# Two attentions reordered: later transpositions in the dilated one, queries, keys, values in the sparse one

## The chip, the cores and the metric

The kernel runs on one core of a Trainium2 chip, as one program. The metric is the device time of one execution in microseconds (us). The engines are called as the profile calls them: PE is TensorE's matrix multiplication and PEld its weight load, DVE is VectorE, ACT is ScalarE, POOL is GpSimd, SP is SyncE, which issues the loads.

## The reference

One sequence of 512 tokens, width 1024, passes through two layers of one kind and one of another, all in float32.

- First kind, twice: `x += 0.5*swiglu(norm(x))`, a mixing part, again `x += 0.5*swiglu(norm(x))`. The mixing part projects to queries, keys and values of 12 heads of 64 and to a pooled part. Each head attends with a mixture of three dilated windows, whose weights come out as one softmax over all 512 keys with a bias by distance:

```
num = sum(wts[i][..., None] * branches[i][0] for i in range(len(branches)))
den = sum(wts[i] * branches[i][2] for i in range(len(branches)))
return (num / den[..., None]).astype(q.dtype)
```

- Second kind, once: a gated MLP over chunks of 128 tokens (`gmlp`), and a sparse attention of 8 heads with 2 groups of keys. That has three outputs, mixed by gates: attention to 31 compressed blocks (each made from 32 keys or values by a small MLP, `cmp_k_w1`, `cmp_k_w2` and the same for v), to selected blocks, and to a window:

```
g = jax.nn.sigmoid(g_raw + gate_b).reshape(B, S, N_GATES, N_KV, GQA, 1)
o = g[:, :, 0] * o_cmp + g[:, :, 1] * o_slc + g[:, :, 2] * o_win
```

With 8 blocks in all and 16 to be selected, every block is selected, so the second and third come out as plain causal attention with different keys and values. A feed-forward and a norm follow.

## The kernel before

Every float32 product is made of three matmuls of rounded halves: `wh*xh + wh*xl + wl*xh` (`mm3`, lines 409 to 413). So each weight tile ("unit", up to 128 x 1024) is loaded by SP (line 305), copied to a rounded high part `wh` by ACT (line 368), and its remainder `wl` is made by DVE (line 375). `unit()` takes the next unit in a fixed list and first splits ahead so that two more are ready; raw tiles, `wh` and `wl` have three buffers each. The list is written in `stages()`, and its order must be that in which the code takes the units. Engines get their instructions in the order that the framework's scheduler works out from the program's order and from what is ready; each engine then runs its own list.

Dilated attention, `mix()` (lines 825 to 1070), called for each of the first two layers: 12 heads of 4 query tiles give 48 tiles, and one loop over steps t (line 1054) runs a software pipeline over them. Step t does the score product of tile t (`qk_step`, line 773 by way of `scores`), normalises tile t-1 (`norm_step`: a reciprocal on DVE and a multiplication on POOL, line 1010), adds the output product of tile t-LP (`pv_step`, line 1034), transposes tile t-LT on PE (`turn_step`, line 1016: four 128 x 128 blocks from the four probability tiles of a head, with the high part copied by ACT, line 1018), takes the softmax of tile t (`exp_step`: DVE line 1003, ACT line 1004) and makes the low part of the transposed tile (`low_step`, line 1023). The first transposition of a head needs the probabilities of all its four tiles. Beside it `beside()` yields small pieces of other projections (late queries, keys and values, then half of the output projection, `out_part`), of which each step takes one or two (line 1067). The probabilities lie in tiles of the tag `work`, of which there are NP.

Sparse attention, `mix2()` (lines 1073 to 1544): in the pool `cm` the kernel projects the inputs of compression (`two_first`), four tiles of queries (`one`, `fill_q`), the keys `ks` and `kw` (`fill_k`), and the values with the gates (`wide`, line 1222); between them `hidden()` (line 1186) yields the pieces of the compression MLP, four units for the keys and four for the values. `blocks()` prepares its inputs `blkh`, `blkl` on POOL, ACT and DVE. Then small weights are loaded and split: `w2` (line 1233, splits in 1235 and 1236) and `ws` with the triangular mask `tril` (lines 1239 to 1244). The pool `cm` closes, a pool `at` opens, and the loop over 64 tiles runs as in `mix()`, with its softmax in line 1277 (DVE), its scores in line 773 and its own LT, LP = 5, 7.

Of the kernel before, what the change touches and what calls it, by code (L numbers as in the profile page):

```python
# [23 lines left out]
ALU = mybir.AluOpType  # L24
AX = mybir.AxisListType

P = 128
# [5 lines left out]
TC = S // P  # L33
# [55 lines left out]
def _u(w, k0, nk, c0, nc):  # L89

    return w[k0 * P : (k0 + nk) * P, c0 : c0 + nc].reshape(nk, P, nc).transpose(1, 0, 2).reshape(P, nk * nc)
# [32 lines left out]
def ffn_units(wg, wu, wd):  # L124
    for t in ffn_plan():
        if len(t) == 2:
            pairs = PHASES[t[0]]
            yield "D", [_u(wd, 2 * pairs[0], 2 * len(pairs), t[1] * P, P)]
        else:
            yield t[2], [  # L130
                np.concatenate([_u(w, 4 * j, 4, (2 * t[1] + i) * P, P) for w in (wg, wu)], 1)
                for i, j in BLOCKS.get(t[2], ())
            ]


def out_units(w):
    for k0 in (0, 4):
        for c0 in range(0, D, 256):
            yield _u(w, k0, 4, c0, 256)


def wide_units(w):
    for k in range(0, 8, 2):
        yield _u(w, k, 2, 0, 512)


def stages(i):
    for l in range(2):
        yield from ffn_units(i["ffn1_w_gate"][l], i["ffn1_w_up"][l], i["ffn1_w_down"][l])
        w = i["w_in"][l]  # L150
        q, k, v = (w[:, 256 + 768 * j : 1024 + 768 * j] for j in range(3))
        yield from wide_units(q[:, :512])
        yield from wide_units(k[:, :512])
        yield _u(w, 0, 8, 0, P)
        yield _u(w, 0, 8, P, P)
        yield from wide_units(v[:, :512])
        for m in (q, k, v):
            yield _u(m, 0, 4, 512, 256)
            yield _u(m, 4, 4, 512, 256)
        yield from out_units(i["w_out"][l])  # L160
        yield from ffn_units(i["ffn2_w_gate"][l], i["ffn2_w_up"][l], i["ffn2_w_down"][l])


    w = i["w_in_2"][0]
    cmp = [_u(i[f"cmp_{n}_w1_2"][0], k0, 4, 0, 256) for n in "kv" for k0 in range(0, 16, 4)]
    q = _by_kv(w[:, 1024:1536])
    v = np.concatenate([w[:, 1920:2048], w[:, 2176:2328]], 1)
    yield from (_u(w, 0, 8, c0, P) for c0 in (1536, 1664))
    yield from (_u(q, 0, 8, j * P, P) for j in range(3))
    yield cmp[0]  # L170
    yield _u(q, 0, 8, 3 * P, P)
    yield cmp[1]
    yield _u(w, 0, 8, 1792, P)
    yield cmp[2]
    yield _u(w, 0, 8, 2048, P)
    yield cmp[3]
    for n, (k0, nk) in enumerate(((0, 3), (3, 3), (6, 2))):
        yield _u(v, k0, nk, 0, 280)
        yield cmp[4 + n]
    yield cmp[7]  # L180
    for c0 in (512, 768, 0, 256):
        yield _u(w, 0, 4, c0, 256)
        yield _u(w, 4, 4, c0, 256)
    wo = i["w_o_2"][0]
    yield from out_units(np.concatenate([wo[:512], _by_kv(wo[512:].T).T]))
    yield from ffn_units(i["w_gate_2"][0], i["w_up_2"][0], i["w_down_2"][0])
# [41 lines left out]
def tile_blocks(tc, A, out):  # L228
    nc = tc.nc
    V, ACT, G, PE = nc.vector, nc.scalar, nc.gpsimd, nc.tensor  # L230

    with (
# [458 lines left out]
        def wide(ncol, kper, after_first=None, between=None):  # L691
            o = [bank() for _ in range(TC)]
            got = None
            for k0 in range(0, KC, kper):
                u = unit()
                for k in range(k0, min(k0 + kper, KC)):
                    c0 = (k - k0) * ncol
                    for t in range(TC):
                        tok = slice(t * P, (t + 1) * P)
                        mm3(o[t][:, :ncol], cut(pair[k], slice(None), tok),  # L700
                            cut(u, slice(None), slice(c0, c0 + ncol)), k == 0, k == KC - 1)
                if k0 == 0 and after_first:
                    got = after_first()
                if between:
                    between()
            return (o, got) if after_first else o
# [69 lines left out]
        def fill_v(dst, src, r):  # L776

            h, l = dst[:, :, 0, :], dst[:, :, 1, :]
            if r is None:
                ACT.activation(h, src, AF.Copy)  # L780
                return low_of(l, src, h)
            else:
                ACT.activation(h, src, AF.Copy, scale=r)
                return V.scalar_tensor_tensor(l, src, r, h.bitcast(F32), op0=ALU.mult, op1=ALU.subtract)
# [39 lines left out]

        def mix(l, nxt):
            with tc.tile_pool(name="mix", bufs=2) as pool:
                NP = 8

                def work(name):
                    return pool.tile([P, 640], F32, name=name, tag="work", bufs=NP)[:, :544]  # L830

# [89 lines left out]
                o, r = wide(512, 2, lambda: row_factor(sums["s"], D, "rf"))  # L921
# [15 lines left out]
                o = wide(512, 2, between=turns(st_q, "q", NQ))  # L937
# [4 lines left out]
                o, mark = wide(512, 2, lambda: state["low"], turns(st_k, "k", NK))  # L942
# [43 lines left out]

                NH = 12
                TURN = 2
                LT, LP = 5, 7
                prob, pt, outp, den = {}, {}, {}, {}  # L990

                def qk_step(t):
# [61 lines left out]
                for t in range(NS + LP):  # L1054
                    if t < NS:
                        sc = qk_step(t)
                    if 0 <= t - 1 < NS:
                        norm_step(t - 1)
                    if 0 <= t - LP < NS:
                        pv_step(t - LP)  # L1060
                    if 0 <= t - LT < NS:
                        turned = turn_step(t - LT)
                    if t < NS:
                        exp_step(t, sc)
                    if 0 <= t - LT < NS:
                        low_step(t - LT, *turned)
                    for _ in range(2 if t < 20 else 1 + (t % 3 == 0)):
                        next(side, None)
                run(side)
                run(out_part(4, second))  # L1070
# [2 lines left out]
        def mix2(nxt):  # L1073
            with tc.tile_pool(name="mix2", bufs=2) as pool:
# [13 lines left out]
                vsw = pool.tile([P, TC, 4, 2, HD], F32R, name="vsw", bufs=1)  # L1088
                gate = pool.tile([P, P], F32, name="gate", bufs=1)[:, : TC * 24].rearrange("p (a b) -> p a b", a=TC)
                caus = pool.tile([P, S], F32, name="caus", bufs=1)  # L1090
                cmpb = pool.tile([P, TC, 32], F32, name="cmpb", bufs=1)
                gateb = pool.tile([P, P], F32, name="gateb", bufs=1)[:, :24]
# [44 lines left out]
                with tc.tile_pool(name="cm", bufs=1) as cm:  # L1137
# [6 lines left out]
                    rho = small.tile([P, TC], F32, name="rho", tag="rfac", bufs=6)  # L1144
# [35 lines left out]
                    blk = blocks(tk, 0)  # L1180
# [5 lines left out]
                    def hidden(b, got):  # L1186

                        o = bank("hid")
                        for k0 in range(0, 16, 4):
                            w = unit()  # L1190
                            for m in range(k0, k0 + 4):
                                mm3(o[0:62, :256], cut(b, slice(None), m), cut(w, slice(None), slice((m - k0) * 256, (m - k0 + 1) * 256)),
                                    m == 0, m == 15)
                            if k0 < 12:
                                yield
                        h = pool.tile([P, 256], F32, name="hid", tag="hid", bufs=2)[0:62]
                        gelu(h, o[0:62, :256], 0.5, 0.5 * c1, work("gq")[0:62, :256])
                        got.append(h)
                        yield
# [11 lines left out]

                    hid = []
                    pieces = hidden(blk, hid)
                    next(pieces)
                    fill_q(qt[3], scaled(one(), rb, -0.125))
                    next(pieces)
                    blk = blocks(tv, 1)
                    for kind in "sw":
                        fill_k(kt[kind], scaled(one(), rb), ACT.copy)
                        next(pieces)  # L1220
                    pieces = hidden(blk, hid)
                    o = wide(280, 3, between=lambda: next(pieces))
                    for t in range(TC):
                        r = rho[:, t : t + 1]
                        fill_v(vsw[:, t], o[t][:, :256].rearrange("p (h d) -> p h d", h=4), r)
                        V.scalar_tensor_tensor(gate[:, t, :], o[t][:, 256:280], r, gateb, op0=ALU.mult, op1=ALU.add)
                    next(pieces)
                    hk, hv = hid

                    tril = cm.tile([P, P], F32, name="tril")  # L1230
                    nc.sync.dma_start(tril, A["consts"][:, C_TRIL : C_TRIL + P])
# [2 lines left out]
                    w = w2.rearrange("p (a b c) -> p a b c", a=2, b=2)  # L1234
                    ACT.activation(w2s[0], w, AF.Copy)
                    V.tensor_sub(w2s[1], w, w2s[0].bitcast(F32))
                    for j in range(2):
# [3 lines left out]
                        w = ws.rearrange("p (a b) -> p a b", a=4)  # L1241
                        V.tensor_tensor(w, w, tril.unsqueeze(1).to_broadcast([P, 4, P]), op=ALU.mult)
                        ACT.activation(wss[0][:, hs], w, AF.Copy)
                        V.tensor_sub(wss[1][:, hs], w, wss[0][:, hs].bitcast(F32))

                    ACT.activation(gate, gate, AF.Tanh, scale=0.5)
                    V.tensor_scalar(gate, gate, 0.5, 0.5, op0=ALU.mult, op1=ALU.add)

# [2 lines left out]
                with tc.tile_pool(name="at", bufs=2) as at:  # L1251
                    KINDS = ("s", "w")
                    LT, LP = 5, 7
# [371 lines left out]
```

## Time and profile before

| | us |
|---|---|
| three runs | 2511.68, 2514.0, 2514.68 |
| median | 2514.0 |
| the profiled execution | 2511.51 |
| its span, first to last instruction | 2509.7 |
| PE busy | 2455.3 (98%) |
| DVE busy | 1970.6 (79%) |
| ACT busy | 1312.8 (52%) |
| POOL busy | 206.3 (8%) |
| DMA | 229.72 MB, mean 92 GB/s |

The busy times are of the one profiled execution. The granted clock of PE is 0.994 of full speed over the span. A "wait" is idle time of an engine just before an instruction, put down to the engine and line whose signal came last. In a timeline a row is an instruction, or several alike that follow each other (x3), with the start, the time from first start to last end, the engine, the line and the tiles (output<-inputs).

### The profile page before, as it was taken

How to read it: one execution, taken by the hardware profiler on the slowest of the kernel's cores; microseconds unless marked ns; L12 is line 12 of the kernel's file. 1: busy time of each engine (PE TensorE's matmuls, PEld its weight loads, DVE VectorE, ACT ScalarE, POOL GpSimd, SP SyncE). 2: the span in 40 equal slices, each digit the busy share in tenths (PEclk: the TensorE clock that was granted, in tenths of full speed). 3: DMA queues.
4: the chain of work that ended last, by engine and by line, in shares of the span. 5: the costliest groups of instructions: out<-in, count | busy, mean ns of one | idle time of the engine just before them, and what ended most of it. 6: DMA issues, size and time to landing. Idle time of an engine off the chain costs nothing.

```text
span 2509.7 us, 39707 instructions
## 1 busy us (share of the span) xinstructions
PE 2455.3 (98%) x15714; PEld 2216.4 (88%) x15714; DVE 1970.6 (79%) x2982; ACT 1312.8 (52%) x2061; POOL 206.3 (8%) x407
## 2 busy tenths in 40 slices
PE   7999999999999999999999999999999999999997
PEld 7999988887999989999988888999988887899996
DVE  8987764798977778877756789887776898987775
ACT  6544443676544455444444776444455775644442
POOL 0000004430000000000003430000000222000000
PEclk9999999999999999999999999999999999999999
DMA  4233232113333332333232113333233211333322
GB/s 178 93 105 101 79 103 84 60 43 105 92 115 105 100 103 84 112 105 101 77 91 84 43 44 116 110 99 106 74 100 108 88 43 43 118 94 109 104 63 78
DMA packets 73338, 229.72 MB, mean 92 GB/s; under 512 B 9536, under 2 KB 9920, under 8 KB 73152
## 3 DMA queue, kind: packets, MB, share of 16 engines
q1 hardware_dynamic: 73152, 227.19, 29.0%
q8 instruction: 123, 2.02, 0.3%
q14 instruction: 63, 0.52, 0.1%
HBM read 225.06 MB, written 2.10 MB: 91 GB/s over the span
## 4 chain that ended last, share of the span: by engine, by line
PE 88%; DVE 7%; ACT 2%; issue 1%; POOL 1%; DMA 1%; DVEq 0%; SPq 0%; ACTq 0%; POOLq 0%
PE x L633 13%; PE x L631 13%; PE x L632 13%; PE dn L411 8%; PE dn L412 8%; PE dn L413 8%; PE mm L411 6%; PE mm L413 6%; PE mm L412 6%; PE ov L1034 1%; DVE wl L375 1%; PE tp L1016 1%; PE mm L773 1%; PE mm L774 1%; PE ov L1323 1%
## 5 line engine op out<-in xcount | busy, mean ns | idle before, releaser
L631 PE MATMUL x<-rh,wh 128*128 128x256 f32 x1600 | 453.9, 284 | 3.2 <-ACT rh L446 2.3
L632 PE MATMUL x<-rl,wh 128*128 128x256 f32 x1600 | 454.3, 284 | 2.7 <-DVE rl L447 2.7
L633 PE MATMUL x<-rh,wl 128*128 128x256 f32 x1600 | 454.2, 284 | 0.7 <-DVE wl L375 0.7
L368 ACT ACTIVATE wh<-wd 128x768 fp32r<-128x768 f32 (+2 forms) x265 | 237.6, 896 | 352.8 <-PE x L632 178.3
L411 PE MATMUL dn<-ah,wh 128*128 128x512 f32 x880 | 343.9, 391 | 0.0
L412 PE MATMUL dn<-al,wh 128*128 128x512 f32 x880 | 343.8, 391 | 0.0
L631 PE MATMUL x<-yh,wh 128*128 128x256 f32 x1200 | 339.8, 283 | 4.0 <-DVE cc L572 3.3
L413 PE MATMUL dn<-ah,wl 128*128 128x512 f32 x880 | 342.3, 389 | 0.0
L633 PE MATMUL x<-yh,wl 128*128 128x256 f32 x1200 | 339.7, 283 | 0.0
L632 PE MATMUL x<-yl,wh 128*128 128x256 f32 x1200 | 339.6, 283 | 0.0
L368 ACT ACTIVATE wh<-wr 128x1024 fp32r<-128x1024 f32 (+1 forms) x178 | 187.6, 1054 | 250.7 <-PE x L632 87.0
L631 PEld LDWEIGHTS x<-rh,wh 128*128 128x128 f32 x1600 | 308.0, 193 | 6.0 <-ACT rh L446 2.5
L632 PEld LDWEIGHTS x<-rl,wh 128*128 128x128 f32 x1600 | 308.2, 193 | 5.4 <-DVE rl L447 3.1
L633 PEld LDWEIGHTS x<-rh,wl 128*128 128x128 f32 x1600 | 308.3, 193 | 1.1 <-DVE wl L375 1.1
L375 DVE TENSOR_TENSOR wl<-wd,wh 128x768 fp32r<-128x768 f32 (+2 forms) x265 | 270.4, 1020 | 43.3 <-ACT wh L368 40.1
L375 DVE TENSOR_TENSOR wl<-wr,wh 128x1024 fp32r<-128x1024 f32 (+1 forms) x178 | 218.5, 1228 | 79.8 <-ACT wh L368 79.1
L631 PEld LDWEIGHTS x<-yh,wh 128*128 128x128 f32 x1200 | 230.2, 192 | 7.9 <-DVE cc L572 4.6
L632 PEld LDWEIGHTS x<-yl,wh 128*128 128x128 f32 x1200 | 230.2, 192 | 2.2
L633 PEld LDWEIGHTS x<-yh,wl 128*128 128x128 f32 x1200 | 230.3, 192 | 0.0
L413 PEld LDWEIGHTS dn<-ah,wl 128*128 128x128 f32 x880 | 165.3, 188 | 35.2
L411 PEld LDWEIGHTS dn<-ah,wh 128*128 128x128 f32 x880 | 165.7, 188 | 31.3
L412 PEld LDWEIGHTS dn<-al,wh 128*128 128x128 f32 x880 | 165.7, 188 | 29.8
(326 smaller groups left out, 5151.1 us busy)
## 6 DMA issues: line engine op xcount, KB each, us to landing
wr<-in_w SPq DMA_DIRECT2D x175, 512.0 KB, 3.6
wd<-in_w SPq DMA_DIRECT2D x120, 384.0 KB, 3.1
wq<-in_w SPq DMA_DIRECT2D x78, 512.0 KB, 3.6
wd<-in_w SPq DMA_DIRECT2D x55, 512.0 KB, 3.6
wd<-in_w SPq DMA_DIRECT2D x40, 256.0 KB, 3.1
x<-in_xT SPq DMA_DIRECT2D x8, 256.0 KB, 6.2
out<-x SPq DMA_DIRECT2D x8, 256.0 KB, 2.0
bias<-in_consts SPq DMA_DIRECT2D x2, 448.0 KB, 3.9
```

The costliest lines, as they stand in the source:

```text
L368: ACT.activation(h[:, :n], src[:, :n], AF.Copy)
L375: state["low"] = V.tensor_sub(l[:, :n], src[:, :n], h[:, :n].bitcast(F32)).ins
L411: PE.matmul(o, w[0], xx[0], start=start, stop=False)
L412: PE.matmul(o, w[0], xx[1], start=False, stop=False)
L413: PE.matmul(o, w[1], xx[0], start=False, stop=stop)
L631: PE.matmul(oo, wh, xh, start=start and j == 0 and c == 0, stop=False, skip_group_check=True)
L632: PE.matmul(oo, wh, xl, start=False, stop=False, skip_group_check=True)
L633: PE.matmul(oo, wl, xh, start=False, stop=c == 3, skip_group_check=True)
L773: PE.matmul(o, q[g][:, cq], k[g][:, ck], start=True, stop=False)
L774: PE.matmul(o, q[g][:, cq], k[2 + g][:, ck], start=False, stop=True)
L1016: PE.transpose(o[:, i * P : (i + 1) * P], prob[h * TC + i][0][:, j * P : (j + 1) * P], ident)
L1034: PE.matmul(o, w, part, start=(j == 0 and n == 0), stop=(j == TC - 1 and n == 1))
```

## The change

In `mix()`: NP from 8 to 9, LT and LP from 5 and 7 to 6 and 8, and the steps with two pieces of side work end at t = 17 instead of 19. In `mix2()`: the fourth query tile comes ahead of the first compression piece, so that the order is queries, one compression piece, the keys `ks`, one piece, the keys `kw`, two pieces; and the loading and splitting of `w2` and `ws` moves ahead of the projection of values and gates. `stages()` lists the units in the new order.

```
@@ -166,14 +166,12 @@
-    yield from (_u(q, 0, 8, j * P, P) for j in range(3))
+    yield from (_u(q, 0, 8, j * P, P) for j in range(4))
     yield cmp[0]
-    yield _u(q, 0, 8, 3 * P, P)
+    yield _u(w, 0, 8, 1792, P)
     yield cmp[1]
-    yield _u(w, 0, 8, 1792, P)
-    yield cmp[2]
     yield _u(w, 0, 8, 2048, P)
-    yield cmp[3]
+    yield from cmp[2:4]
...
-                NP = 8
+                NP = 9
...
-                LT, LP = 5, 7
+                LT, LP = 6, 8
...
-                    for _ in range(2 if t < 20 else 1 + (t % 3 == 0)):
+                    for _ in range(2 if t < 18 else 1 + (t % 3 == 0)):
                         next(side, None)
...
                     pieces = hidden(blk, hid)
-                    next(pieces)
                     fill_q(qt[3], scaled(one(), rb, -0.125))
                     next(pieces)
                     blk = blocks(tv, 1)
                     for kind in "sw":
                         fill_k(kt[kind], scaled(one(), rb), ACT.copy)
                         next(pieces)
-                    pieces = hidden(blk, hid)
-                    o = wide(280, 3, between=lambda: next(pieces))
-                    for t in range(TC):
...
-                        V.scalar_tensor_tensor(gate[:, t, :], o[t][:, 256:280], r, gateb, op0=ALU.mult, op1=ALU.add)
                     next(pieces)
-                    hk, hv = hid

                     tril = cm.tile([P, P], F32, name="tril")
...
                         V.tensor_sub(wss[1][:, hs], w, wss[0][:, hs].bitcast(F32))

+                    pieces = hidden(blk, hid)
+                    o = wide(280, 3, between=lambda: next(pieces))
+                    for t in range(TC):
...
+                        V.scalar_tensor_tensor(gate[:, t, :], o[t][:, 256:280], r, gateb, op0=ALU.mult, op1=ALU.add)
+                    next(pieces)
+                    hk, hv = hid
                     ACT.activation(gate, gate, AF.Tanh, scale=0.5)
```

## Rows read from the trace of the kernel before

**Rows 1.** The page, part 1: busy time and share of the span

```profile
PE 2455.3 (98%) x15714; PEld 2216.4 (88%) x15714; DVE 1970.6 (79%) x2982; ACT 1312.8 (52%) x2061; POOL 206.3 (8%) x407
```

**Rows 2.** Busy time by stretch: us, PE, PEld, DVE, ACT, POOL, clock, DMA

```profile
455.00:585.00 130.00, 124.75 (x751) 105.53 (x750) 105.81 (x247) 93.67 (x194) 46.78 (x90) 1.00 0.14 45
...
1886.00:1960.00 74.00, 69.96 (x421) 61.69 (x420) 52.25 (x96) 39.56 (x59) 6.18 (x8) 0.98 0.44 140
```

**Rows 3.** Waits of PE, whole run: us in total, times, longest

```profile
PE tp L1016 <- POOL prob L1010: 7.1, 8, 2.2
...
PE mm L773 <- DVE stat L1277: 3.2, 2, 3.0
...
PE hid L412 <- DVE wl L375: 2.3, 1, 2.3
...
PE hid L411 <- ACT blkh L1175: 0.5, 1, 0.5
```

**Rows 4.** Timeline of PE, first layer's loop: start us, us, engine, line

```profile
458.70 0.40 PE L773 MATMUL mm<-qk 128*128 128x512 f32 x1
...
460.59 0.40 PE L773 MATMUL mm<-qk 128*128 128x512 f32 x1
...
461.06 0.49 PE L1016 MATMUL tp<-consts,prob 128*128 128x128 f32 x3
...
463.70 0.33 PE L1016 MATMUL tp<-consts,prob 128*128 128x128 f32 x1 [2.15 <-POOL prob L1010]
```

**Rows 5.** Timeline of POOL and of DVE, the same stretch

```profile
461.90 2.42 POOL L1010 TENSOR_SCALAR prob<-prob,stat 128x512 f32<-128x512 f32 x2
...
461.86 1.23 DVE L375 TENSOR_TENSOR wl<-wr,wh 128x1024 fp32r<-128x1024 f32 x1 [0.19 <-ACT wh L368]
```

**Rows 6.** Timeline of PE, end of the first layer's loop

```profile
570.12 0.48 PE L773 MATMUL mm<-qk 128*128 128x512 f32 x1
...
576.18 0.33 PE L1016 MATMUL tp<-consts,prob 128*128 128x128 f32 x1 [0.93 <-POOL prob L1010]
...
582.83 0.42 PE L1034 MATMUL ov<-ptl,vhl 128*128 128x512 f32 x1
```

**Rows 7.** Timeline of DVE and of PE, ahead of the sparse loop

```profile
1955.45 0.22 DVE L1249 TENSOR_SCALAR gate<-gate,consts 128x8 f32<-128x8 f32 x1
...
1957.62 0.69 DVE L1236 TENSOR_TENSOR w<-w,w 128x512 fp32r<-128x512 f32 x1 [1.94 <-ACT w L1235]
...
1961.05 0.29 DVE L1277 CUSTOM_DVE_ANT_0 prob<-mm,caus 128x128 f32<-128x128 f32 x1
...
1961.74 0.37 PE L773 MATMUL mm<-kw,q 128*128 128x128 f32 x1 [3.00 <-DVE stat L1277]
```

**Rows 8.** The chain that ended last, in order of time: start us, us, what

```profile
1951.57 5.36 DMA w<-in_cmp_w
```

**Rows 9.** Busy time by stretch (columns of rows 2), after the two holes

```profile
1916.00:1919.00 3.00, 2.35 (x13) 2.25 (x14) 3.00 (x4) 0.63 (x1) 0.00 (x0) 0.75 0.38 100
...
1919.00:1922.00 3.00, 3.00 (x11) 2.35 (x10) 2.91 (x5) 2.31 (x3) 0.00 (x0) 0.68 1.00 348
...
1962.00:1968.00 6.00, 6.00 (x28) 5.74 (x28) 4.91 (x18) 5.19 (x17) 3.74 (x4) 0.50 0.17 43
...
1961.00:1975.00 14.00, 12.53 (x78) 11.33 (x79) 11.57 (x42) 11.68 (x37) 6.33 (x7) 0.76 0.08 21
```

**Rows 10.** Timeline of SP, DVE and PE in the value projection

```profile
1933.77 0.33 SPq L305 DMA_DIRECT2D wr<-in_w  x1
...
1937.71 1.03 DVE L375 TENSOR_TENSOR wl<-wr,wh 128x840 fp32r<-128x840 f32 x1 [0.51 <-ACT wh L368]
...
1944.78 1.22 DVE L375 TENSOR_TENSOR wl<-wr,wh 128x1024 fp32r<-128x1024 f32 x1 [3.93 <-ACT wh L368]
...
1938.99 0.29 PE L412 MATMUL mm<-wl,yh 128*128 128x280 f32 x1
```

**Rows 11.** Timeline of DVE, the split that the compression hole ends with

```profile
1915.38 2.36 DVE L375 TENSOR_TENSOR wl<-wr,wh 128x1024 fp32r<-128x1024 f32 x2
```

More of the change, by code (lines that the diff above doesn't have):

```diff
@@ L1220, in mix2 @@
                         next(pieces)
-                    pieces = hidden(blk, hid)
-                    o = wide(280, 3, between=lambda: next(pieces))
-                    for t in range(TC):
-                        r = rho[:, t : t + 1]
-                        fill_v(vsw[:, t], o[t][:, :256].rearrange("p (h d) -> p h d", h=4), r)
-                        V.scalar_tensor_tensor(gate[:, t, :], o[t][:, 256:280], r, gateb, op0=ALU.mult, op1=ALU.add)
                     next(pieces)
-                    hk, hv = hid
                     tril = cm.tile([P, P], F32, name="tril")
@@ L1244, in mix2 @@
                         V.tensor_sub(wss[1][:, hs], w, wss[0][:, hs].bitcast(F32))
+                    pieces = hidden(blk, hid)
+                    o = wide(280, 3, between=lambda: next(pieces))
+                    for t in range(TC):
+                        r = rho[:, t : t + 1]
+                        fill_v(vsw[:, t], o[t][:, :256].rearrange("p (h d) -> p h d", h=4), r)
+                        V.scalar_tensor_tensor(gate[:, t, :], o[t][:, 256:280], r, gateb, op0=ALU.mult, op1=ALU.add)
+                    next(pieces)
+                    hk, hv = hid
                     ACT.activation(gate, gate, AF.Tanh, scale=0.5)
```

## The prediction

> **What bounds the kernel now.** I read the page first: TensorE (PE) is busy 98% of the span, so a change can only win where PE waits or where its clock falls [rows 1]. The table of stages shows where that is. The dilated attention of the first layer (455 to 585 us) has PE busy 124.75 of 130 us with VectorE (DVE) at 105.81, that is 81%; the projections ahead of the sparse attention (1886 to 1960) have 69.96 of 74 [rows 2]. The second layer is built like the first, and the counts of the whole run below hold both. Then I read who made PE wait. Over the whole run the transpositions of line 1016 waited 7.1 us in 8 waits for the normalised probabilities of GpSimd (POOL), the scores of line 773 waited 3.0 us at one place for the sparse softmax, and the compression matmuls `hid` waited 2.3 us for a low weight part `wl` and 0.5 us for `blkh` [rows 3]. These 12.9 us are the change's targets; the rest of PE's span is matmuls that stay as they are.
>
> **Dilated attention, twice.** No instruction is added or removed; the transposition and the output product of a tile move one step later in the order, and a ninth probability buffer holds the tile that lives a step longer. Buffers: before, the tile of step 4h is last read in step 4h+8, ahead of that step's softmax, and eight buffers suffice; after, it is last read in step 4h+9, and nine suffice in the same way. So I price the buffer at nothing; its cover is that the read stands ahead of the write in the step, as now.
>
> The first wait: PE reaches the transpositions of the first head at 461.06, does three and waits 2.15 us for the fourth, until 463.70 [rows 4]. POOL started that probability at 461.90, while DVE ran a split of weights beside it, and two such operations took 2.42 us [rows 5]. A step of PE's work there is what lies between two score products, 458.70 to 460.59, so 1.89 us [rows 4]. With one more step ahead of the transposition the 2.15 becomes 0.26; I take 1.9 saved. What comes late next is nothing of POOL's: its order, norm by norm, is the old one.
>
> The last wait: at the end of the loop PE waits 0.93 us for the last head's probability [rows 6]. From the first score product shown there to the last output product 12.7 us pass for eight steps, 1.6 us each [rows 6]; one step more in hand covers the 0.93, and I take 0.8. The two smaller POOL waits of a layer are what is left of half the 7.1, some 0.5 [rows 3]; I take 0.3. So 3.0 a layer, 6.0 in both. Ends: nothing, and all 7.1. The value is near the upper end because two waits of known length make most of it and a measured step of PE's work stands against each.
>
> The side work: two pieces a step up to step 17 instead of 19, then four in three steps. Counted out, the side work is one piece behind from step 19 on and ends at step 46 instead of 45; the loop has 56 steps instead of 55, so the steps without side work stay nine. Its transpositions of late queries and keys stay at steps 6 and 14, and the output projection begins at step 23 instead of 22, just as the second pair's output comes a step later. Its loads on SyncE's queue (SP) follow it by less than a step. Cost nothing, hidden by PE's own work; without cover the extra step of the drain costs its 1.6 us a layer [rows 6].
>
> **Sparse attention, the hole at its start.** Before, the small weights of compression and gating (`w2`, `ws`) are loaded and split after the value projection. DVE is done with the gates at 1955.67, stands still for ScalarE's (ACT) copy of `w2`, works off `w`, `ws` and `wsl` from 1957.62, and only then takes the first softmax at 1961.05; PE, whose score banks are full, stands for 3.00 us until 1961.74 [rows 7]. Behind DVE's wait is a load of 5.36 us [rows 8]. Then the granted clock is 0.50 from 1962 to 1968 [rows 9]: six microseconds at the lower level, 1.2 GHz, lose 3.0. So the hole costs up to 6.0.
>
> The change moves all this ahead of the value projection. The first softmax can then follow the gates, 1961.05 - 1955.67 = 5.4 us earlier. It now may meet a split of weights on DVE, 1.2 us, two in 2.36 [rows 11]; I take 4.2 saved. Ends: nothing, if another wait ends there, and 6.0. That the engines can follow I read from 1961 to 1975: DVE 11.57 and ACT 11.68 busy of 14.0 us [rows 9], tight but not full.
>
> What the moved work meets: SP issues a weight load at 1933.77, after which I expect `w2` and `ws` [rows 10]. In program order their splits now stand ahead of the second value weights' split (DVE, 1937.71 to 1938.74), whose low part PE first uses at 1938.99: 0.25 us to spare [rows 10]. The program's scheduler puts what is ready first, and DVE stands 3.93 us before 1944.78, more than the 3.4 us of the moved work [rows 7, 10]. I take 0.5 lost; ends 0 and 4.9 of wait (the rival below) with the clock's 3.0.
>
> **Sparse attention, the compression hole.** The fourth queries now go ahead of the first compression piece, so `blkh` is no longer waited for (0.5). But the next split of weights stands behind the same query work on DVE and is done no earlier: it starts at 1915.38 [rows 11]. Before, it holds the second compression piece; after, the first keys. PE has the same work ahead of it, so the 0.48 is only added to the 2.30. Nothing gained. The clock: 0.75 and 0.68 in the two stretches of 3 us after that wait [rows 9], 0.75 + 0.96 = 1.7 us lost now; a longer wait may lose up to the 3.0 of the other hole. I take 0.5 more.
>
> The Trainium skill ("TensorE: Matmul & The Clock Gate", section "Why this matters for your kernels") asks for no idle gaps of some length between bursts of matmuls, since the clock then falls to half; by that, one long hole is worse than a short and a middling one, and this part of the change speaks for a loss. The trace agrees as far as it goes: 0.50 after the wait of 3.00 us, 0.75 and 0.68 after that of 2.30 [rows 9]. By it the term is 1.3 instead of 0.5, and the sum 0.8 less.
>
> **Sum.** 6.0 + 4.2 - 0.5 - 0.5 = 9.2 us. The profiled execution took 2511.5 us (span 2509.7), so 2502.3 by its own time; the median of the runs shown, 2514.0, stands 2.5 above it, so 2504.8. Some 0.2% (5.0 us) is what a measurement of this kernel can tell from no change.
>
> **Rivals.**
> - Moved preparation holds up the value weights. If `w2`'s load takes its 5.36 us from 1934.1 and the whole chain of 3.4 us and the split of 1.03 follow in line, the split ends at 1943.9: PE waits 4.9 us and loses up to 3.0 of clock, against 4.2 saved; with the 6.0 of the dilated part and the 0.5 of the compression hole, 2512. If only `w` (0.69) stands ahead: 1941.2, a wait of 2.2 and half the clock's loss; 2508. For it: ACT and DVE run in order, 0.25 us to spare. Against: the free time behind. Chance 0.20, centre 2510. That the scheduler undoes the new order belongs here.
> - The dilated waits only move, say to DVE, which at 81% is close behind PE. Then 3.2 us are left from the sparse part: 2510.8. Chance 0.15.
> - The one longer hole loses clock as the other does: 1.3 instead of 0.5, so 2505.6. Chance 0.10. The Trainium skill's page on the clock gate, named above, would have it so.
> - Slower: DVE and ACT, not PE, set the pace of both attentions. PE's waits are then shadows, their removal saves nothing, and the pipeline is only a step longer: 2 x 1.6 us of drain, and 1.0 for the two small sparse losses; 2518.2. It decides if DVE or ACT are close to full; 81% and 11.6 of 14.0 speak against it. Chance 0.07.
>
> **How the numbers follow.** My case has 0.48. Low: both upper ends, 13.1 us, give 2500.9, and the fastest run shown lies 2.3 below its median: 2498.6. High: the first two rivals up to 2512. Under 2509 lie my case, the clock's, half of the first rival and a third of the second: 0.73. Over 2519 lies less than half of the slower rival: 0.04.
>
> **What would show it.** Right: the waits of line 1016 for POOL fall from 7.1 to about 1 us; DVE goes from the gates to the softmax without `w`, `ws`, `wsl` between; line 773 has no 3.0 us wait, and the clock stays 1.00 behind it. Wrong: a wait of `mm` for `wl` in the value projection, a low clock there, or waits of the same length in the dilated attention with another releaser.

## The result and the profile after

The changed kernel took 2498.4 us (median of 4 runs, 2497.9 to 2498.7), the kernel before 2513.7 beside it: ratio 0.9945, 95% interval [0.9934, 0.9957]. That is 15.3 us less, where 9.2 were forecast, and 0.2 us under the 2498.6 that the prediction works out as its low end. In a later series the same two stood at 2500.2 and 2511.2, 11.0 us apart, ratio 0.9954 [0.9938, 0.9971]. The profiled execution took 2498.5 us (span 2496.7), against 2511.5 before: 13.0 less.

The first part of the page and two stretches of the changed kernel, set like those of [rows 2] (loop of the first dilated layer; projections ahead of the sparse loop; columns as there):

```profile
PE 2450.6 (98%) x15714; PEld 2213.2 (89%) x15714; DVE 1971.9 (79%) x2982; ACT 1312.2 (53%) x2061; POOL 205.0 (8%) x407
```

```profile
449.80:579.80 130.00, 127.82 (x777) 109.13 (x776) 108.31 (x253) 94.35 (x195) 48.50 (x96) 1.00 0.15 46
...
1878.00:1952.00 74.00, 70.93 (x431) 62.56 (x432) 57.09 (x113) 43.34 (x69) 7.45 (x10) 0.98 0.48 144
```

PE is busier by 3.07 us of the first 130 and by 0.97 of the 74. (The first stretch begins 4 us earlier in its stage than that of before; begun at the same point, from 453.97 to 583.97, PE is busy 127.82 us as well.) The work is the same, so it ends earlier. Where, the first norm matmul `tst` of each stage tells. Before, timeline of PE:

```profile
368.59 0.95 PE L491 MATMUL tst<-ones,ss 128*128 128x1 f32 x8
...
611.80 0.95 PE L491 MATMUL tst<-ones,ss 128*128 128x1 f32 x8
...
1885.53 0.95 PE L491 MATMUL tst<-ones,ss 128*128 128x1 f32 x8
...
2125.97 0.95 PE L491 MATMUL tst<-ones,ss 128*128 128x1 f32 x8
```

After (lines of `mix()` and later are two lower than before):

```profile
367.56 0.95 PE L489 MATMUL tst<-ones,ss 128*128 128x1 f32 x8
...
607.45 0.95 PE L489 MATMUL tst<-ones,ss 128*128 128x1 f32 x8
...
1877.83 0.94 PE L489 MATMUL tst<-ones,ss 128*128 128x1 f32 x8
...
2112.94 0.95 PE L489 MATMUL tst<-ones,ss 128*128 128x1 f32 x8
```

So the first dilated layer takes 239.89 us instead of 243.21 (611.80 - 368.59), the sparse one 235.11 instead of 240.45. The same subtraction for all kernels, in us:

| profiled execution of | first FFN | dilated 1 | dilated 2 | sparse | last FFN |
|---|---|---|---|---|---|
| before | 345.45 | 243.21 | 243.14 | 240.45 | 370.59 |
| after | 343.97 | 239.89 | 239.96 | 235.11 | 370.61 |
| after, second execution | 345.46 | 239.93 | 239.94 | 235.46 | 371.88 |
| dilated half alone | 343.97 | 239.97 | 239.93 | 239.13 | 371.30 |
| sparse half alone | 345.44 | 243.21 | 243.13 | 237.24 | 371.20 |
| preparation's move alone | 345.46 | 243.21 | 243.10 | 236.63 | 370.66 |
| order alone | 345.43 | 243.21 | 243.12 | 241.26 | 372.06 |
| after, eight buffers | 343.97 | 240.81 | 240.85 | 235.50 | 371.93 |
| before, nine buffers | 345.32 | 243.39 | 244.85 | 240.73 | 370.59 |
| late turns one piece later | 345.60 | 239.61 | 239.68 | 235.43 | 371.91 |
| query products first | 345.45 | 239.97 | 239.94 | 232.57 | 370.64 |
| the last two together | 343.96 | 239.72 | 239.68 | 232.28 | 370.57 |

Of the profile's 13.0 us, 6.5 lie in the dilated layers, 5.3 in the sparse one and 1.5 in the first feed-forward part, which the change doesn't touch. Ahead of the first of these matmuls the changed kernel took 0.45 us longer (23.59 instead of 23.14).

Waits of PE over the whole run after, against [rows 3]:

```profile
PE tp L858 <- POOL st L850: 1.9, 2, 0.9
PE hid L409 <- ACT wh L366: 1.5, 1, 1.5
PE mm L409 <- ACT gq L1107: 1.4, 2, 1.1
...
PE kc L409 <- issue: 0.8, 1, 0.8
...
PE tp L1014 <- POOL prob L1008: 0.4, 2, 0.2
...
PE mm L771 <- DVE stat L1275: 0.2, 1, 0.2
```

The wait for POOL's probabilities fell from 7.1 to 0.4, the 3.0 at the sparse scores went. New are two waits of 0.9 at the late queries' transposition, waits of 1.5 and 1.1 ahead of the sparse loop, and one of 0.8 in its first steps.

**The first wait of the dilated loop**, against [rows 4, 5]: PE, then POOL and DVE.

```profile
461.89 0.49 PE L1014 MATMUL tp<-consts,prob 128*128 128x128 f32 x3
...
462.58 0.33 PE L1014 MATMUL tp<-consts,prob 128*128 128x128 f32 x1 [0.21 <-POOL prob L1008]
...
465.61 0.33 PE L858 MATMUL tp<-consts,st 128*128 128x128 f32 x1 [0.94 <-POOL st L850]
```

```profile
460.84 1.69 POOL L1008 TENSOR_SCALAR prob<-prob,stat 128x512 f32<-128x512 f32 x1
...
463.17 1.32 DVE L373 TENSOR_TENSOR wl<-wr,wh 128x1024 fp32r<-128x1024 f32 x1
...
463.39 1.21 POOL L846 TENSOR_TENSOR ra<-st,cos 128x32 f32<-128x32 f32 x1
```

2.15 us became 0.21 (0.26 was forecast). The 0.94 behind it is POOL again: a rope operation that takes 0.25 us elsewhere took 1.21 beside DVE's split, and the late queries wait for it.

**The sparse loop's start**, against [rows 7]. DVE:

```profile
1929.40 1.02 DVE L373 TENSOR_TENSOR wl<-wr,wh 128x840 fp32r<-128x840 f32 x1
...
1930.68 0.68 DVE L1232 TENSOR_TENSOR ws<-ws,tril 128x512 f32<-128x512 f32 x1
...
1946.28 1.23 DVE L373 TENSOR_TENSOR wl<-wr,wh 128x1024 fp32r<-128x1024 f32 x1 [0.48 <-ACT wh L366]
1947.76 0.22 DVE L1247 TENSOR_SCALAR gate<-gate,consts 128x8 f32<-128x8 f32 x1
1947.98 0.29 DVE L1275 CUSTOM_DVE_ANT_0 prob<-mm,caus 128x128 f32<-128x128 f32 x1
```

The softmax follows the gates at once. The value weights' split went ahead of `ws`, so the moved work held up no weights.

**The clock behind the waits**, columns as in [rows 2]; before, then after:

```profile
1961.00:1964.00 3.00, 2.25 (x9) 1.93 (x10) 2.77 (x13) 2.97 (x7) 0.00 (x0) 0.65 0.35 87
1964.00:1967.00 3.00, 3.00 (x16) 3.00 (x15) 3.00 (x10) 2.74 (x11) 2.74 (x2) 0.50 0.00 0
1967.00:1970.00 3.00, 3.00 (x23) 2.97 (x21) 1.15 (x6) 1.51 (x7) 1.95 (x4) 0.71 0.03 8
```

```profile
1908.00:1911.00 3.00, 2.96 (x7) 1.95 (x8) 2.97 (x4) 1.91 (x4) 0.00 (x0) 0.55 0.30 63
1911.00:1914.00 3.00, 3.00 (x13) 2.39 (x12) 2.94 (x5) 0.47 (x1) 0.00 (x0) 0.88 0.79 257
1944.00:1958.00 14.00, 13.22 (x111) 12.04 (x110) 13.42 (x40) 11.76 (x35) 5.60 (x6) 1.00 0.44 137
```

Taking what is missing to 1.00 times the stretch, the hole at the loop's start lost 1.05 + 1.50 + 0.87 = 3.4 us of clock, and none after. The compression hole lost 1.7 before [rows 9] and 1.35 + 0.36 = 1.7 after.

### The profile page after: what moved, and what is told of

Its sections match the earlier page's. It is cut to its first block, busy times and chain, and to the rows that moved or that the text cites. A ratio compares the mean times of both kernels' runs of the same rounds, so it can differ in the third digit from the quotient of the medians.

```text
span 2496.7 us, 39692 instructions
## 1 busy us (share of the span) xinstructions
PE 2450.6 (98%) x15714; PEld 2213.2 (89%) x15714; DVE 1971.9 (79%) x2982; ACT 1312.2 (53%) x2061; POOL 205.0 (8%) x407
## 4 chain that ended last, share of the span: by engine, by line
PE 87%; DVE 8%; ACT 3%; issue 1%; POOL 1%; DMA 0%; DVEq 0%; SPq 0%; ACTq 0%; POOLq 0%
PE x L631 13%; PE x L629 13%; PE x L630 13%; PE dn L409 8%; PE dn L410 8%; PE dn L411 8%; PE mm L409 5%; PE mm L410 5%; PE mm L411 5%; PE ov L1032 2%; PE tp L1014 1%; DVE wl L373 1%; PE mm L771 1%; PE mm L772 1%; ACT wh L366 1%
```

## The experiments

**1. The halves, and the parts of the sparse half**

Four kernels beside each other; the kernel before took 2511.98 us there (26 runs).

```
dilated half alone, on the kernel before:
-                NP = 8
+                NP = 9
-                LT, LP = 5, 7
+                LT, LP = 6, 8
-                    for _ in range(2 if t < 20 else 1 + (t % 3 == 0)):
+                    for _ in range(2 if t < 18 else 1 + (t % 3 == 0)):
sparse half alone: the same lines undone in the changed kernel
preparation's move alone, on the kernel before (from tril to wss):
                     next(pieces)
+                    tril = cm.tile([P, P], F32, name="tril")
...
                     pieces = hidden(blk, hid)
                     o = wide(280, 3, between=lambda: next(pieces))
order alone: the sparse half with the same block put back behind the values
```

> Only the dilated half of the change (nine buffers, transposition and output product a step later, side work halved from step 18). Theory, the step covers the waits for late probabilities: each of the two dilated stages is 3.2 us shorter, as in the changed kernel, and the time falls by 6.5 us; the sparse stage keeps its length. Rival, the dilated gain needs the sparse half or is scatter: under 3 us.

> Only the sparse half (order of units, preparation of w2 and ws ahead of the values). Theory, the halves add up: the sparse stage is 5.3 us shorter, the two dilated ones keep their length, the time falls by 5.3 us. Rival, the halves meet somewhere (a load queue, the clock): the sparse stage differs by over 1 us from that of the changed kernel.

> Only the preparation of w2 and ws moves ahead of the values; units in the old order. Theory, the hole before the first sparse softmax and its low clock were the whole sparse gain: the 3.0 us wait of line 773 and the 0.50 clock behind it are gone, 5 us less. Rival, the order of queries and keys made the gain: less than 1.5 us.

> Only the order of queries, keys and compression pieces changes; w2 and ws stay behind the values. Theory: the wait of 3.0 us of line 773 stays, the compression hole shrinks by about 0.9 us and a new wait of 1.3 us at the values takes it back, so 0 with an end at 1 either way. Rival, the order made the sparse gain: 4 us less or more.

| | us, median | to before | ratio, 95% |
|---|---|---|---|
| dilated half | 2504.16 | -7.8 | 0.9969 [0.9958, 0.9981] |
| sparse half | 2505.35 | -6.6 | 0.9975 [0.9965, 0.9985] |
| preparation's move | 2507.26 | -4.7 | 0.9980 [0.9972, 0.9989] |
| order | 2512.10 | +0.1 | 1.0001 [0.9992, 1.0010] |

The two halves' differences sum to 14.4 us; the change itself gave 15.3 and 11.0 in its two series. Each dilated layer is 3.2 us shorter with the dilated half alone, within 0.1 us of the changed kernel's.

The sparse stage did not follow as expected. With the dilated half alone it took 239.13 us, 1.3 less than before, though nothing in it is changed. With the sparse half alone it took 237.24 us, which is 3.2 less instead of 5.3 and 2.1 more than in the changed kernel, past the 1 us that was set as the rival's sign. That profile is the slowest of its nine runs (2509.26 us), and the clock is enough to explain it: in the loop the granted clock was 0.57 from 2053 to 2061 us, a loss of 3.4 us that the changed kernel's two profiles don't have.

In the sparse part the preparation's move makes most of the gain, 4.7 us by the medians and 3.8 by the stage, where 5 was expected; the new order is worth nothing alone. With the move the clock is 1.00 behind the place of the old hole, but in this profile too it fell later in the loop, so that the stage lost 5.1 us of clock, as before:

```profile
2020.00:2060.00 40.00, 37.73 (x253) 33.93 (x252) 35.77 (x111) 31.50 (x91) 9.07 (x14) 0.92 0.17 53
```

Move and order together gave 6.6, which is 1.9 more than the move alone. The intervals overlap and the two profiles don't show it (237.24 and 236.63); the listed clocks go that way, 0.996 in five of nine runs against 0.994 in seven of eleven. So what the order is worth beside the move stays open. Waits of PE from 1885 to 1965 us, preparation's move alone, then order alone:

```profile
PE hid L412 <- DVE wl L375: 2.3, 1, 2.3
PE kc L411 <- issue: 0.9, 1, 0.9
PE hid L411 <- ACT blkh L1175: 0.5, 1, 0.5
```

```profile
PE mm L771 <- DVE stat L1275: 2.5, 1, 2.5
PE hid L409 <- ACT wh L366: 1.5, 1, 1.5
PE mm L409 <- ACT gq L1107: 1.2, 1, 1.2
PE mm L409 <- ACT wh L366: 0.4, 1, 0.4
```

With the move the wait at the scores is gone. The order has 1.9 us of waits in the compression hole in place of 2.8, and makes a new wait of 1.2: two compression pieces now stand back to back, and the value projection waits for their bank until the gelu `gq` has read it.

**2. The buffer**

```
after with eight:         -NP = 9   +NP = 8
before with nine:         -NP = 8   +NP = 9
```

> The changed kernel with eight probability buffers in place of nine. If the ninth is what the later transposition needs, the softmax of one tile in each head waits until the transposition of the step after, VectorE shows waits for TensorE at the softmax's line, and the dilated stages are 1 to 3 us a layer longer than 239.9. If eight would have done: 239.9 and no such wait.

> The kernel before with nine probability buffers and nothing else. If the buffer alone helps (a softmax that waited for a buffer to come free), the dilated stages fall by 0.9 us from 243.2 as they rose by 0.9 when the changed kernel was given eight; if it only serves the later transposition, 243.2 as before and the same 7.1 us of waits of the transpositions for GpSimd.

With eight, the dilated layers took 240.81 and 240.85, 0.9 more each, just under the 1 to 3 expected. The waits of DVE in the loop (455 to 580 us) have a line that the changed kernel lacks there:

```profile
DVE prob L1001 <- PE tp L1014: 1.3, 3, 0.7
```

That is the softmax waiting for the transposition that frees its buffer; the kernel before has such waits too (1.7 us in 4). With nine in the kernel before, the first layer took 243.39; the second took 244.85, of which 1.7 is a fall of the clock at 1391 us (0.88 and 0.55 in two stretches of 3), so 243.15 without it. The transpositions still waited:

```profile
PE tp L1016 <- POOL prob L1010: 6.6, 6, 2.1
```

So the buffer gives nothing by itself; the step later gives 2.4 a layer without it and 3.3 with it. Single runs took 2501.7 and 2512.8 us.

**3. The same program once more: the first feed-forward part**

> The changed kernel once more, unaltered, for a second profiled execution. In the profiles so far the first feed-forward takes 1.5 us less wherever the dilated half is in (344.0 against 345.4 us), though its waits on TensorE are the same: the granted clock falls to 0.50 for some 3 us after 46 us in the four other programs, and stays 1.00 in these two. Theory 1, the fall belongs to the execution or to the program's chance phase and not to the edit: another execution of the same program may show it, the sparse stage (235.1 us in the first profile) may come out up to 2 us longer, and runs scatter by 1 to 3 us with the mean clock. Theory 2, the edit takes it away: clock 1.00 there again, 344.0. Time by both: 2498.4, plus or minus 1.

2500.23 us (2497.82 to 2502.35). The clock in one stretch of the first feed-forward part: before, after, and after in the second execution.

```profile
47.00:50.00 3.00, 3.00 (x17) 3.00 (x16) 3.00 (x4) 0.00 (x0) 0.00 (x0) 0.50 0.27 52
```

```profile
47.00:50.00 3.00, 3.00 (x27) 3.00 (x27) 3.00 (x4) 0.60 (x3) 0.00 (x0) 1.00 0.05 5
```

```profile
47.00:50.00 3.00, 3.00 (x16) 3.00 (x15) 3.00 (x4) 0.00 (x0) 0.00 (x0) 0.50 0.28 45
```

The same program with the same waits (1.8, 0.9 and 0.45 us between 41 and 46 us) lost the clock in one execution and kept it in the other: 345.46 against 343.97 us. The kernel with eight buffers, profiled in the same series as the second execution, kept it (343.97). So theory 1 holds, and these 1.5 us are no gain of the change. The last feed-forward part differs alike, 371.88 against 370.61.

**4. Does TensorE set the pace? The late transpositions one piece later**

```
-                TURN = 2
+                TURN = 3
```

> The changed kernel, with the late queries and keys transposed one piece of side work later. Theory, that TensorE sets the pace and its waits are what the dilated stages lose: the wait of 0.9 us a layer for the late queries' rope on GpSimd, which came up where the old wait had been, goes; the stage falls from 239.9 to some 239.0 us, the time from 2498.4 to 2496.5. Rival, another engine sets the pace and the wait is its shadow: the 0.9 turns up at another instruction, stage 239.9, time 2498.4.

The stages fell by 0.3, to 239.61 and 239.68, not by 0.9; the time was 2499.67 us, 0.6 under the changed kernel beside it, which the scatter covers. Waits of PE in the first loop (455 to 580 us):

```profile
PE tp L1014 <- DVE qk L751: 0.9, 2, 0.7
...
PE tp L1014 <- DVE ptl L1021: 0.4, 1, 0.4
PE tp L1014 <- POOL prob L1008: 0.2, 1, 0.2
```

The 0.94 is gone, and waits for DVE have come up in its place, 1.3 us instead of 0.3; all waits in this stretch sum to 1.9, against 1.8 after the change. So the rival holds for the waits: DVE stands close behind. That the stage is 0.3 shorter all the same is not in the waits. Counted from each start to the next without them, the first layer's transpositions and output products took 45.25 us instead of 45.60; why is not shown.

**5. One step between transposition and product**

The next kernel also has the edit of experiment 6, which doesn't touch the dilated part.

```
-                LT, LP = 6, 8
+                LT, LP = 6, 7
```

> Four query products first, and the output product of the dilated part back at seven steps while the transposition stays at six: one step between transposition and product in place of two, and a loop one step shorter. Theory, TensorE sets the pace and the extra step of drain costs: if the low part of the transposed tile is ready within one step, the stage gains up to the 1.6 us of a step, 238.4; if it is not, TensorE waits for it at the output product in most of the 48 tiles, and the stage is longer than 239.9 by 48 times that wait. Rival, that nothing depends on the step: 239.9.

The layers took 244.39 and 244.09 us, 4.4 and 4.2 more than with eight (one run, 2507.6 us). But PE's waits in the first loop rose by only about 1.6. The rest shows in PE's groups of instructions there (busy us, mean ns), with seven steps and with eight:

```profile
L1032 PE MATMUL ov<-ptl,vhl 128*128 128x512 f32 x48 | 20.9, 435 | 0.1
L1032 PE MATMUL ov<-pth,vhl 128*128 128x512 f32 x48 | 20.1, 418 | 0.5 <-ACT pth L1016 0.3
```

```profile
L1032 PE MATMUL ov<-pth,vhl 128*128 128x512 f32 x48 | 19.5, 405 | 0.1
L1032 PE MATMUL ov<-ptl,vhl 128*128 128x512 f32 x48 | 19.3, 402 | 0.0
```

With no slack the scheduler pulls the two products of a tile apart and sets transpositions and others between; PE changes between transpositions, output products and other products 215 times instead of 166, and the products are 33 and 13 ns longer on the mean, 2.2 us for 48. Counted from each start to the next without waits, over the whole layer, the output products took 25.7 us instead of 23.6 and the transpositions 22.7 instead of 22.1; with 1.8 more of waits that is the 4.4. That the mixed order is what makes them longer is argued from these rows. Neither branch of the theory came: PE did not wait in most of the tiles, and the shorter loop gained nothing. Two steps between are needed, and the longer drain is cheap beside them.

**6. The compression hole**

```
+                    oq += [one(), one()]
-                    for j in range(2):
+                    for j in range(4):
                         fill_q(qt[j], scaled(oq[j], rb, -0.125))
-                    fill_q(qt[2], scaled(one(), rb, -0.125))
...
                     pieces = hidden(blk, hid)
-                    fill_q(qt[3], scaled(one(), rb, -0.125))
```

> The changed kernel, with all four query products issued ahead of the first query work, so that the next weight splits stand ahead of that work on VectorE and ScalarE. Theory, the compression hole is the split standing in line behind the query work: the hole of some 2.2 us and the clock lost behind it (1.7 us in the first profile) go, at most 3.9 us, so 2494.5 to 2496.5, and no wait for a low weight part is left there. Rival, the hole only moves (to a bank of the queries, or to the transposed inputs of compression): 2498.4, with the same sum of waits between 1876 and 1912 us.

2497.73 us (2496.74 to 2498.41), beside 2500.23 of the changed kernel. The sparse stage took 232.57 us, 2.5 to 2.9 less than with the change alone, and its clock stayed 1.00 throughout. Waits of PE from 1878 to 1960 us:

```profile
PE mm L411 <- DVE wl L373: 1.2, 1, 1.2
PE kc L409 <- issue: 0.8, 1, 0.8
PE mm L409 <- ACT gq L1107: 0.6, 1, 0.6
PE hid L410 <- DVE wl L373: 0.2, 1, 0.2
```

They sum to 2.8 instead of 3.8 after. The theory holds in its cause. The time lies above the 2494.5 to 2496.5 expected, though 2.5 below the changed kernel beside it, and a wait for a low weight part of 1.2 us is left, against the expectation. More of the gain is the clock (1.7) than the waits (1.0).

**7. Both further edits together**

> The two edits that gained by their stages, together: all four query products ahead of the query work in the sparse part, and the late transpositions one piece later in the dilated one. Stages: dilated 239.6 to 239.7 us each (239.9 without the second edit), sparse 232.6 (235.1 to 235.5 without the first). If both hold, 2.8 + 2 x 0.3 = 3.4 us under the changed kernel on the same chip, some 2495 to 2497; rival, that the medians do not follow the stages because the clock's falls in single executions outweigh them: 2498 to 2500.

2496.76 us (2494.47 to 2498.02), ratio to before 0.9943 [0.9927, 0.9960]; stages 239.72, 239.68 and 232.28.

> The kernel with both further edits once more, in more rounds. By the stages (239.7, 239.7 and 232.3 us against 239.9, 239.9 and 235.1 to 235.5 of the changed kernel) it is 3.2 us faster than the changed kernel, whose eight runs so far have a median of 2498.6: 2495.5, with single runs from 2494 to 2499 as the clock's falls come and go. If instead the sparse stage's gain belonged to one lucky execution: 2498 and a sparse stage of 234 or more.

2497.36 us (2495.54 to 2498.66), ratio 0.9945 [0.9932, 0.9959]; stages 239.71, 239.61 and 232.60. By the stages it is 3.2 us under the changed kernel; by the medians (2497.3 of nine runs, 2498.6 of eight) 1.3, and the runs overlap. The stages hold in both executions; that the whole time is shorter by 3.2 isn't shown. The kernel of experiment 5, which has the sparse edit too, took 234.88 us for the sparse stage: it lost nothing at the compression hole either, but 3.4 us of clock later in the loop (from 2053 us on).

## Why the prediction was right, and where it was not

**Dilated part: right, and its size too.** 3.0 a layer was taken, 3.3 and 3.2 came. The waits for POOL's probabilities fell by 3.35 a layer: the first wait went from 2.15 to 0.21 us, the last one (0.93) is gone, the loop's extra step shows no cost of its own. That "what comes late next is nothing of POOL's" failed: the late queries' rope on POOL was next, 0.9 a layer. What paid for about half of it is the waits for `qk`, which fell from 1.6 to 0.6 over both layers and stood in no term either. That the total came so near is in part these errors cancelling, which is luck. The ninth buffer was rightly priced at nothing and is needed: 0.9 a layer.

**Sparse part: right in its places, too small in its sum.** 3.2 was forecast; the stages give 5.3 between the first two profiles and 4.4 as means (240.1 of three executions with the old start and none of the change's sparse edits, 235.8 of five with both). In the first two profiles it can be counted out: PE's waits ahead of the loop fell from 3.0 + 2.3 + 0.5 to 1.5 + 1.1 + 0.8 + 0.4, so by 2.0, and the clock's loss from 5.1 to 1.7, so by 3.4; 5.4 in all. By the same means as above, the waits of the whole stage fell by 1.7 and the clock's loss by 3.3.

- "I take 4.2 saved" is the mis-sized term in the first two profiles. The hole's 3.0 and its clock's 3.4 both went (the forecast's 3.0 of clock left out the ends of the fall), so the upper end would have been right there. The 1.2 was taken off for a split of weights that the softmax may meet on DVE; the split is there (1946.28), but PE still had products to do and didn't wait.
- But the hole of the one profile that the prediction had was the largest of three. The lines below show it in the two other executions with the same start: 2.0 and 2.2 us, each followed by a loss of 1.7 of clock, so 3.7 and 3.9 in all against 6.4. Against the mean of the three, 4.7, the 4.2 was nearly right, and part of the clock's gain by the means is that it fell less often later in the loop, near 2055 us. Whether the change has to do with that is not shown.
- The compression hole shrank, 2.8 to 1.9, where it was forecast to grow and to cost 0.5 more of clock; the clock lost 1.7 as before.
- The moved preparation's -0.5 was due to the value weights; those weren't late. In its place came waits of 1.1 (the bank behind `gq`) and 0.8 (`kc`), named nowhere in the prediction. The first is in the order alone, the second in the move alone.

Waits of PE, whole run, dilated half alone, then the kernel before with nine buffers:

```profile
PE mm L773 <- DVE stat L1277: 2.0, 1, 2.0
```

```profile
PE mm L773 <- DVE stat L1277: 2.2, 1, 2.2
```

**The median.** The 2.5 us added to the profiled execution's own time came from three runs. In later series the kernel before stood at 2511.98, 2511.21, 2511.20 and 2511.18, so the profiled execution was an ordinary one, and the forecast 2502.3 by its own time was the better figure. With 10.9 us from the stages instead of 9.2 that is 2500.6; the first series, at 2498.4, was below it. Its listed clocks are 0.996 in three of four runs, where those of the kernel before are mostly 0.994 in the later series; that the clock fell less often in these runs is likely, but only one of them was profiled.

**The rivals.** No value matmul waited for a low part: the first fell. The second, that the waits move to DVE, is true of the next step only (experiment 4). For the third, the compression hole lost no more clock than before. The Trainium skill ("TensorE: Matmul & The Clock Gate", section "Why this matters for your kernels") tells to avoid idle gaps of some length between bursts of matmuls, and the prediction worked out from it that one longer wait loses more. The trace has no longer wait, but 1.5 and 0.4 us with the same loss of 1.7, so that was not put to the test here. The slower rival fell with the dilated half alone.

## What to carry to other kernels

- Price a hole by its wait and by the clock behind it, and take both when the cause is moved away; over half of the sparse gain, and of experiment 6's, was clock. Take both from more than one profile: the same hole cost 6.4, 3.7 and 3.9 us.
- A pipeline's distance has a right size on each side; in this loop one step more before the transposition gave 3.3 us a layer, one step less behind it cost 4.4, with few waits to show for it. Run both.
- Compare stages between fixed instructions, and list the clock of each, before a microsecond or two in a single execution is put down to an edit.

## What was not expected of the hardware

The clock's falls are not fixed to a program. In the profiles each stage with falls lost some 1.7, 3.4, 5.1 or 6.8 us in all, and between executions of the same work the figure changed: the first feed-forward part lost 0, 1.7 or 3.4, the last one 1.7 or 3.4, and around 2055 us in the sparse loop the clock fell in six of the programs and not in the others, though PE's waits there, 1.2 us and some of 0.3, are much the same in all. Nor did the same wait always cost clock: after the compression hole's 2.3 us the kernel before lost 1.7, but that with the dilated half alone lost none, 1.00 from 1908 to 1950 us. The clocks listed for the runs go with their times (the changed kernel's were 0.996 at 2497.8 us and 0.994 at 2502.4), so these falls are likely most of the scatter, some 3 to 5 us for one kernel, about a third of what the change is worth.

POOL's small operations lose as much beside DVE's splits as its large ones: the rope's took 1.21 us beside a split and 0.25 without, the normalisation 1.69 and 0.69, so each about 1.0 more.
